# A feature-major SSM and MLP block: the MLP's up-projection in seven products of halves, and gated unit and MLP one half of the tokens after the other

## The chip, the cores and the metric

The kernel runs on one core of a Trainium2 chip. The metric is the device time of one execution in microseconds (us). TensorE (PE, with its weight loads PEld) does the matrix products, VectorE (DVE), ScalarE (ACT) and GpSimd (POOL) the elementwise work, SyncE (SP) issues the transfers between device memory and the core's on-chip memory (SBUF). Products accumulate in PSUM, eight banks of 128 x 512 float32. Each engine executes its own instructions in order and waits for others at semaphores.

## The reference

Two blocks follow each other on a stream x of 2048 tokens by 1024 features in float32. The part that is changed lies in the first block:

```
x = x + a * sigmoid(g)              # a, g = split(y @ w_glu), y: the SSM mixer's gelu output
h = rmsnorm(x, norm_ffn)
a = relu(h @ w1)                    # w1: 1024 x 4096
x = x + (a * a) @ w2                # w2: 4096 x 1024
gate = sigmoid(rmsnorm(x, norm_ple) @ ple_gate_w)
x = x + (p @ ple_w) * gate
return rmsnorm(x, norm_final)       # goes into the second block
```

The second block (band attention, a matrix LSTM, a long convolution, an output projection) and the SSM recurrence itself are not touched.

## The kernel before

The stream lies feature-major: eight tiles x0 to x7 of 128 features by 2048 tokens, worked on in four blocks n of 512 tokens. Every float32 operand of a large product is split into a high and a low float16 part, and each tile of 128 input features takes three matmuls of 128 x 128 by 512 columns: high by high, high weight by low data, low weight by high data (`product`, L252 to L262, matmul on L260). So the third matmul is the first that needs the weight's low part.

A weight tile of 128 x 2048 arrives in two halves `ws` (transfer issued by SP, L1923) and is split by `Weights.prepare` in four quarters: ACT writes a quarter's high part (L1962), then VectorE the low part (`w<-ws,w`, a scalar_tensor_tensor by the helper on L59). That makes five jobs: job q issues the low part of quarter q-1 and the high part of quarter q. When the low part of the second or fourth quarter is issued, that half's buffer goes to the next tile's load. `step(n)` (L245) is called between products and issues up to n jobs of norms that are pending and one job of the weights; `get(i)` issues at once whatever of tile i is left. The order of issue is the order in which each engine works: nothing is scheduled later.

Gated unit (`glu`, L364): a unit (m, n) makes 128 output features for one block, 96 matmuls in two banks; ACT takes the sigmoid (L373), VectorE multiplies (L59) and adds to x (L41), ACT squares for the next norm (L281, L284). For each of the first six tiles m its four blocks n follow one another, and the split of tile m+1 is queued after the first of the four. Two units of tile 0 are begun in the mixer.

MLP (`mlp`, L395): 16 pieces c of 256 hidden features. `up(c, n)` takes 2 x 48 matmuls of two banks; ACT does relu (L414) and the high part of the square (L416), VectorE the square and the low part (L41). `down` of the pair before takes 8 groups of 6 matmuls, each evicted by VectorE into x (L59: `x<-dn,x`). For pieces 2 to 13 all four blocks use a piece's weights in turn.

Per-layer gate (`ple`, L465): 24 matmuls of gate weights (pg) and 6 of the per-layer input (pp) per unit, in two passes over n. Norms of the blocks are jobs: sums of squares through a matmul (nps, L301), rsqrt in small VectorE steps, a matmul that spreads the result over partitions (nsp, L317), and per tile a scalar_tensor_tensor (nt, L59), a cast on ACT (L333) and a subtraction. PSUM is divided among names: four banks "b" (ga, up, pg), three "a" (dn, pp), one "c" (nps, nsp).

## Time and profile before

| what | value |
|---|---|
| median of 3 runs | 3357.24 us (3356.96, 3357.24, 3362.16) |
| span of the profiled execution | 3364.8 us |
| TensorE matmuls busy | 3272.9 us, 97% |
| VectorE busy | 1905.9 us, 57% |
| ScalarE busy | 1059.0 us, 31% |
| moved by DMA | 189.01 MB, mean 56 GB/s |
| gated unit, from its first full unit | 318.9 to 632.8 us |
| MLP | 632.8 to 1971.8 us |

No time of the profiled execution beside its span is given; the span stands for it. Busy times are shares of the whole span, over stages with different limits; the windows by stage below separate them. Matmuls are pipelined, so their recorded durations overlap and the distance from one to the next is what one costs. A number in square brackets on a timeline row is the idle time of that engine before the row, and what ended it.

### The profile page before, as it was taken

The numbers are of one execution on the slowest core, as the hardware profiler recorded it, in microseconds if no ns is written. First come the engines' busy times: TensorE is split into PE (matmuls) and PEld (weight loads), VectorE is DVE, ScalarE is ACT, GpSimd is POOL, SyncE is SP. The second block draws the span as 40 slices with busy tenths as digits, with TensorE's granted clock in tenths as the row PEclk, the third lists the DMA queues.
The fourth block names the chain that finished last, engine by engine and source line by source line (L and its number), as shares of the span: only waits on it lengthen the run. The fifth ranks groups of instructions, "written<-read, shape, count | busy, mean of one in ns | idle before, by whom it ended". The sixth has DMA issues, their size and how long they took to land. (4 is left out here: it accounts for less than half of the span.)

```text
span 3364.8 us, 44052 instructions
## 1 busy us (share of the span) xinstructions
PE 3272.9 (97%) x17524; PEld 1690.9 (50%) x17524; DVE 1905.9 (57%) x4109; ACT 1059.0 (31%) x2293; POOL 165.8 (5%) x162
## 2 busy tenths in 40 slices
PE   7778999999999999999999999999999999999999
PEld 6664444444444444444444444464554445666644
DVE  8995222664444444444444582756657885677742
ACT  8995111321111111111112243331221224555610
POOL 0000111000000000000000223300000000000000
PEclk9888999999999999999999999999999999999999
DMA  4113101100000000000001011032111224322232
GB/s 155 36 49 133 32 26 32 44 1 26 26 26 26 27 30 26 26 26 26 31 26 38 1 51 38 14 129 95 51 66 67 91 88 127 98 80 79 82 141 85
DMA packets 125870, 189.01 MB, mean 56 GB/s; under 512 B 32800, under 2 KB 83936, under 8 KB 121952
## 3 DMA queue, kind: packets, MB, share of 16 engines
q1 hardware_dynamic: 121056, 177.81, 16.3%
q10 hardware_dynamic: 4608, 8.39, 0.6%
q8 instruction: 138, 2.26, 0.3%
q14 instruction: 68, 0.56, 0.1%
HBM read 142.64 MB, written 43.52 MB: 55 GB/s over the span
## 5 line engine op out<-in xcount | busy, mean ns | idle before, releaser
L260 PEld LDWEIGHTS <-w 128*128 128x128 f16 x9792 | 959.0, 98 | 1156.5 <-issue 8.2
L260 PE MATMUL up<-h,w 128*128 128x512 f16 x2880 | 632.1, 379 | 1.7 <-DVE w L59 1.7
L260 PE MATMUL dn<-hid,w 128*128 128x512 f16 x2880 | 632.0, 379 | 1.4 <-DVE x L59 1.4
L59 DVE SCALAR_TENSOR_TENSOR x<-dn,x 128x512 f32<-128x512 f32 x512 | 346.4, 688 | 182.7 <-PE dn L260 180.2
L414 ACT ACTIVATE r<-up 128x512 f32<-128x512 f32 x128 | 76.3, 596 | 975.0 <-PE up L260 974.9
L41 DVE TENSOR_TENSOR q<-r 128x512 f32<-128x512 f32 x128 | 88.5, 692 | 475.3 <-ACT r L414 475.3
L260 PE MATMUL ga<-y,w 128*128 128x512 f16 x1536 | 336.6, 382 | 3.4 <-DVE w L59 2.1
L41 POOL TENSOR_TENSOR ss<-ss,sq 128x512 f32<-128x512 f32 x84 | 113.1, 1347 | 2044.6 <-ACT sq L284 2043.5
L977 PE MATMUL oz<-oz,h 128*128 128x512 f16 x768 | 189.6, 385 | 0.0
L260 PE MATMUL pg<-h,w 128*128 128x512 f16 x768 | 170.8, 379 | 0.0
L59 DVE SCALAR_TENSOR_TENSOR w<-ws,w 128x512 f16<-128x512 f32 x220 | 157.0, 728 | 23.5 <-ACT w L1962 23.5
L1351 PE MATMUL fo<-mx,wo 128*128 128x512 f16 x768 | 167.4, 379 | 0.0
L260 PE MATMUL wide<-w,h 128*128 128x512 f16 x768 | 166.9, 379 | 0.0
L260 PE MATMUL mqk<-h,w 128*128 128x512 f16 x768 | 165.9, 379 | 0.0
L260 PEld LDWEIGHTS <-h 128*128 128x128 f16 x1152 | 112.3, 98 | 99.5 <-DVE gif L59 4.0
L59 DVE SCALAR_TENSOR_TENSOR acc<-u,par,acc 128x512 f32<-128x512 f32 x232 | 159.1, 744 | 0.0
L59 DVE SCALAR_TENSOR_TENSOR sg<-ga,sg 128x512 f32<-128x512 f32 x32 | 22.1, 691 | 214.1 <-ACT sg L373 214.1
L1962 ACT ACTIVATE w<-ws 128x512 f16<-128x512 f32 x220 | 129.2, 616 | 10.3 <-DMA ws<-w 6.2
L1351 PEld LDWEIGHTS <-wo 128*128 128x128 f16 x768 | 75.0, 98 | 88.6
L977 PEld LDWEIGHTS <-h 128*128 128x128 f16 x768 | 71.2, 99 | 68.0 <-issue 3.0
L284 ACT ACTIVATE sq<-x 128x512 f32<-128x512 f32 x84 | 52.7, 630 | 162.7 <-DVE x L41 126.8
L41 DVE TENSOR_TENSOR hid<-q,hid 128x512 f16<-128x512 f32 x128 | 88.6, 692 | 15.4 <-DVE q L41 2.7
(340 smaller groups left out, 3621.5 us busy)
## 6 DMA issues: line engine op xcount, KB each, us to landing
ws<-w SPq DMA_DIRECT2D x64, 512.0 KB
ws<-wd SPq DMA_DIRECT2D x34, 512.0 KB
xu<-xu SPq DMA_DIRECT2D x8, 1024.0 KB
tm<-rz_scr SPq DMA_DIRECT2D x64, 128.0 KB
x<-xT SPq DMA_DIRECT2D x8, 1024.0 KB
ws<-wglu SPq DMA_DIRECT2D x16, 512.0 KB
x_s<-x SPq DMA_DIRECT2D x8, 1024.0 KB
qk_s<-o SPq DMA_DIRECT2D x32, 256.0 KB
```

Of the source, the lines that this page charges most:

```text
L41: f = lambda: (eng or self.nc.vector).tensor_tensor(out=out, in0=in0, in1=in1, op=op)
L59: f = lambda: self.nc.vector.scalar_tensor_tensor(out=out, in0=in0, scalar=s, in1=in1, op0=op0, op1=op1)
L260: self.nc.tensor.matmul(out=ps, lhsT=wk[p], rhs=xk[q], start=(first and i == 0 and j == 0), stop=(last and i == n - 1 and j == 2))
L284: self.nc.scalar.activation(out=sq, in_=x, func=ACT.Square, **kw)
L414: nc.scalar.activation(out=r, in_=ps, func=ACT.Relu, scale=0.5 / WS)
L977: nc.tensor.matmul(out=d["bank", g], lhsT=x[:, k, s], rhs=y[:, c], start=(k == 0 and j == 0), stop=(k == 7 and j == 2))
L1351: self.nc.tensor.matmul(out=self.begun[m, n], lhsT=w[:, x, c], rhs=y[:, k], start=(k == 0 and j == 0), stop=(k == KT - 1 and j == 2))
L1962: nc.scalar.activation(out=hi, in_=src, func=ACT.Copy, scale=scale)
```

## The change

Tokens are worked on in two halves of two blocks. In a half, gated unit, norm and MLP follow each other; wglu, w1 and w2 are loaded and split once for each half. The gated unit's order is half, tile m, block n, and the split of the next tile is queued after the first of the two units of a tile.

The up product of a piece (two blocks of tokens, two halves of 512 input features, two tiles of 128 hidden features) is a product of 2 by 2 blocks, and is made by Strassen's scheme in Winograd's form: seven products of 12 matmuls on sums and differences of operands, in four banks a, c, b, d, with some sums made in the banks and five additions on VectorE. The data's seven combinations are made once for each half by `norm_pair` (`part`, 28 jobs); those of the second half, and one of the first, are parked in device memory and fetched. The weights' seven are made for each piece and half by `combine`: four sums and seven low parts on VectorE, seven high parts on ACT. The square that is subtracted from is made on ACT now. `down` takes both blocks at once: 16 groups of 6 matmuls. The norms ahead of the per-layer gate are made in the middle of the MLP for blocks 0 and 1 (parked and fetched) and in the gate for 2 and 3, and the gate takes blocks 0 and 1 before 2 and 3. Comments are dropped.

The core of the diff; the removed bodies of `glu` and `mlp` stand in the listing above. `fetch` and `fetch_normed` issue transfers from the parking places, `operand` and `combined` name places.

```diff
+        tiles = [(self.a["wglu"][i], WS) for i in range(KT)] * 2
...
-        w = self.weights.get(m)
+        w = self.weights.get(KT * (n // 2) + m)
...
         return ps
     def glu(self, begun):
-        nc = self.nc
+        nc, W = self.nc, self.weights
+        self.places()
         def unit(m, n):
             if m == 0 and n < len(begun):
                 ps = self.gated(n, m, [KT - 1], begun[n])
             else:
-                ps = self.gated(n, m, range(KT), between=lambda: self.step(4))
+                ps = self.gated(n, m, range(KT), between=lambda: self.step(2))
             sg = self.temp(name="sg")
             nc.scalar.activation(out=sg, in_=ps[1], func=ACT.Sigmoid, scale=1 / WS)
             self.stt(sg, ps[0], 1 / WS, sg, ALU.mult, ALU.mult)
             x = self.x[m][:, self.blk(n)]
             self.add(x, x, sg)
             self.squares(m, n, m == 0)
-            self.step(4)
...
+            self.step(2)
+        for half in range(2):
+            for m in range(KT):
+                for n in (2 * half, 2 * half + 1):
+                    unit(m, n)
+                    if n % 2 == 0:
+                        i = KT * half + m + 1
+                        if i < 2 * KT:
+                            W.prepare(i)
+                        else:
+                            self.combined(0)
+            self.norm_pair(half)
...
+    def norm_pair(self, half):
+        nc = self.nc
+        na, nb = 2 * half, 2 * half + 1
...
+        def normed(x, k, n):
+            self.stt(x, self.x[k][:, self.blk(n)], self.gain[:, 0, k:k + 1], self.rb[n % 2], ALU.mult, ALU.mult)
+        def put(x, o, k):
+            away = half or o == 6
+            if away:
+                t = self.parked(at)
+                hi, lo = t[:, 0], t[:, 1]
+            else:
+                hi, lo = (self.operand(o, k, p) for p in range(2))
+            nc.scalar.copy(out=hi, in_=x)
+            def rest():
+                self.sub(lo, x, hi)
+                if away:
+                    dst = self.hop_s[o if half else 7, :, k].rearrange("p (a b) -> p a b", a=2)
+                    nc.sync.dma_start(out=dst, in_=t)
+            low.append(rest)
+        def part(k, q):
+            if low:
+                low.pop()()
+            if q == 0:
+                v["x"] = self.tmp.tile([128, TB], F32, name="nt", tag="n0")
+                v["y"] = self.tmp.tile([128, TB], F32, name="nt", tag="n1")
+            x, y, z = v["x"], v["y"], third
+            if q == 0:
+                normed(x, k, na)
+                put(x, 0, k)
+            elif q == 1:
+                normed(y, k, nb)
+                self.sub(x, y, x)
+                put(x, 1, k)
+            elif q == 2:
+                normed(z, k + 4, nb)
+                put(z, 5, k)
+            elif q == 3:
+                self.sub(y, z, y)
+                put(y, 4, k)
+            elif q == 4:
+                self.sub(x, z, x)
+                put(x, 2, k)
+            elif q == 5:
+                normed(y, k + 4, na)
+                put(y, 3, k)
+            elif q == 6:
+                self.sub(x, y, x)
+                put(x, 6, k)
+        jobs += [lambda k=k, q=q: part(k, q) for k in range(4) for q in range(7)] + [lambda: part(0, 7)]
+        self.pending += [(("pair", half), j) for j in jobs]
...
+        def finish(j, src, r, i, n):
+            t = self.hid[j % 2][i]
+            c = slice(TB * n, TB * n + TB)
+            nc.scalar.activation(out=r, in_=src, func=ACT.Relu, scale=0.5 / WS)
+            nc.scalar.activation(out=t[:, 2, c], in_=r, func=ACT.Square)
+            nc.scalar.activation(out=r, in_=r, func=ACT.Square)
+            later.append(lambda: self.sub(t[:, 3, c], r, t[:, 2, c]))
+        def up(j, steps):
+            ops = W.get(self.at_up[j])
+            u, v = self.rows[2 * (j % 2):2 * (j % 2) + 2]
+            ps = {}
+            for o, name in enumerate("acbadcd"):
+                first = name not in ps
+                if first:
+                    ps[name] = self.bank("b", 4, name="up")
+                for k in range(4):
+                    for p, q in ((0, 0), (0, 1), (1, 0)):
+                        nc.tensor.matmul(out=ps[name], lhsT=ops[o][:, p, 128 * k:128 * k + 128],
+                                         rhs=self.operand(o, k, q), start=(first and k == 0 and p + q == 0),
+                                         stop=(k == 3 and p == 1), skip_group_check=not first)
+                self.step(steps[o])
+                flush()
+                if o == 0:
+                    nc.scalar.copy(out=u, in_=ps["a"])
+                elif o == 2:
+                    self.add(u, ps["b"], u)
+                    self.add(v, ps["c"], u)
+                elif o == 3:
+                    finish(j, ps["a"], self.temp(name="r"), 0, 0)
+                elif o == 4:
+                    self.add(v, ps["d"], v)
+                    finish(j, v, v, 1, 1)
+                elif o == 5:
+                    c = self.temp(name="r")
+                    self.add(c, ps["c"], u)
+                    finish(j, c, c, 0, 1)
+                elif o == 6:
+                    self.add(u, ps["d"], u)
+                    finish(j, u, u, 1, 0)
+        def down(j, between=None):
+            hi, lo = W.get(self.at_dn[j])
+            half, c = j // NPIECE, j % NPIECE
+            for q in range(2):
+                if q and between:
+                    between()
+                for n in range(2):
+                    for m in range(4 * q, 4 * q + 4):
+                        ps = self.bank("a", 3, name="dn")
...
+                        x = self.x[m][:, self.blk(2 * half + n)]
+                        self.stt(x, ps, 4 / WS, x, ALU.mult, ALU.add)
+                        if later:
+                            flush()
+                        if c == NPIECE - 1:
+                            self.squares(m, 2 * half + n, m == 0)
+                        if (m % 2 or j == 2 * NPIECE - 1) and not (q and n and between):
+                            self.step(0 if c < NPIECE - 1 else 1)
...
+        second = lambda j: W.prepare(self.at_dn[j], lambda: w2)
+        self.fetch(6, 7)
+        few, many = (1, 0, 1, 0, 1, 0, 0), (1,) * 7
+        for j in range(2 * NPIECE):
+            c = j % NPIECE
+            if c == 0:
+                self.combined(j + 1)
+            else:
+                second(j - 1)
+            up(j, few if c else many)
+            if c == NPIECE - 1:
+                if j < 2 * NPIECE - 1:
+                    while self.pending:
+                        self.step()
+                    for o in range(7):
+                        self.fetch(o, o)
+                else:
+                    while self.pending:
+                        self.step()
+                    self.fetch_normed()
+            if c:
+                if c < NPIECE - 1:
+                    self.combined(j + 1)
+                down(j - 1, (lambda: second(j)) if c == NPIECE - 1 else None)
+            if c == NPIECE - 1:
+                if j < 2 * NPIECE - 1:
+                    self.combined(j + 1)
+                else:
+                    for i in range(2):
+                        W.prepare(self.at_p + i)
+                    W.prepare(self.at_p + 2, lambda: self.slot(2, [128, 2, 2048], F16, "p0"))
+                down(j)
+                if j < 2 * NPIECE - 1:
+                    self.norm_parked()
+        for n in (2, 3):
+            self.norm(n, 1, late=4)
...
-        order = [(m + e, n) for m in (0, 2) for n in range(NB) for e in range(2)]
+        order = [(m + e, 2 * h + n) for h in range(2) for m in (0, 2) for n in range(2) for e in range(2)]
...
+    def combine(self, i, place):
+        k, nc = self.k, self.k.nc
+        scale = self.tiles[i][1]
+        out = self.ready[i] = []
+        low = []
+        tmp = {}
+        at = lambda r, c: self.loaded[i, c][:, 512 * r:512 * r + 512]
...
+        def source(q):
+            if q in (0, 3, 6):
+                return at(*((0, 0), (0, 1), (1, 1))[q // 3])
+            if q == 1:
+                x = tmp["s"] = new()
+                k.add(x, at(1, 0), at(1, 1))
+            elif q == 2:
+                x = tmp["s"]
+                k.sub(x, x, at(0, 0))
+            elif q == 4:
+                x = new()
+                k.sub(x, at(0, 0), at(1, 0))
+            else:
+                x = tmp["s"]
+                k.sub(x, at(0, 1), x)
+            return x
+        def part(q):
+            if low:
+                low.pop()()
+            if q == 7:
+                return
+            src = source(q)
+            t = place(q)
+            out.append(t)
+            nc.scalar.activation(out=t[:, 0], in_=src, func=ACT.Copy, scale=scale)
+            def rest():
+                k.stt(t[:, 1], src, scale, t[:, 0], ALU.mult, ALU.subtract)
+                j = {4: 0, 6: 1}.get(q)
+                if j is not None:
+                    del self.loaded[i, j]
+                    self.load(i + 1, j)
+            low.append(rest)
+        self.jobs += [(i, lambda q=q: part(q)) for q in range(8)]
```

Three places show how instructions stand. Operands carry buffer numbers; what an instruction waits for stands in brackets.

VectorE at a tile boundary of the gated unit, before: sg and x are a unit's product and sum, w_3638 the low parts of the tile that follows tile 3.

```order
L59 SCALAR_TENSOR_TENSOR sg_3652<-ga0_3600,sg_3652 128x512 [waits Activation_49]
L41 TENSOR_TENSOR x3_2902<-x3_2902,sg_3652 128x512 [waits DVE_49]
L59 SCALAR_TENSOR_TENSOR w_3638<-ws_3459,w_3638 128x512 [waits DMAHW2_49]
L59 SCALAR_TENSOR_TENSOR w_3638<-ws_3459,w_3638 128x512 [waits Activation_49]
L59 SCALAR_TENSOR_TENSOR sg_3715<-ga0_3661,sg_3715 128x512 [waits Activation_49]
L41 TENSOR_TENSOR x3_2902<-x3_2902,sg_3715 128x512 [waits DVE_49]
L59 SCALAR_TENSOR_TENSOR w_3638<-ws_3522,w_3638 128x512 [waits DMAHW3_49]
L59 SCALAR_TENSOR_TENSOR w_3638<-ws_3522,w_3638 128x512 [waits Activation_49]
L59 SCALAR_TENSOR_TENSOR sg_3777<-ga0_3724,sg_3777 128x512 [waits Activation_49]
L41 TENSOR_TENSOR x3_2902<-x3_2902,sg_3777 128x512 [waits DVE_49]
L59 SCALAR_TENSOR_TENSOR sg_3834<-ga0_3784,sg_3834 128x512 [waits Activation_49]
L41 TENSOR_TENSOR x4_2904<-x4_2904,sg_3834 128x512 [waits DVE_49]
```

The last unit of tile 3 is the one of sg_3777, and sg_3834 is the first unit of the next tile. After, at the same boundary; here w_3302 is the tile after tile 3:

```order
L59 SCALAR_TENSOR_TENSOR sg_3257<-ga0_3207,sg_3257 128x512 [waits Activation_49]
L41 TENSOR_TENSOR x3_2902<-x3_2902,sg_3257 128x512 [waits DVE_49]
L59 SCALAR_TENSOR_TENSOR sg_3316<-ga0_3264,sg_3316 128x512 [waits Activation_49]
L41 TENSOR_TENSOR x3_2902<-x3_2902,sg_3316 128x512 [waits DVE_49]
L59 SCALAR_TENSOR_TENSOR w_3302<-ws_3199,w_3302 128x512 [waits DMAHW2_49]
L59 SCALAR_TENSOR_TENSOR w_3302<-ws_3199,w_3302 128x512 [waits Activation_49]
L59 SCALAR_TENSOR_TENSOR w_3302<-ws_3205,w_3302 128x512 [waits DMAHW3_49,Activation_49]
L59 SCALAR_TENSOR_TENSOR w_3302<-ws_3205,w_3302 128x512 [waits Activation_49]
L59 SCALAR_TENSOR_TENSOR sg_3384<-ga0_3334,sg_3384 128x512 [waits Activation_49]
L41 TENSOR_TENSOR x4_2904<-x4_2904,sg_3384 128x512 [waits DVE_49]
```

The four low parts stood behind the second and the third of four units; they stand now behind the second of two, and sg_3384 right after them is the unit that uses the tile.

VectorE where an up product ends and down begins, before (hid and q: squared relu; dn: a bank of down):

```order
L59 SCALAR_TENSOR_TENSOR x7_2910<-dn_9052,x7_2910 128x512 [waits PE_49]
L41 TENSOR_TENSOR q_9088<-r_9086 128x512 [waits Activation_49]
L41 TENSOR_TENSOR hid_9060<-q_9088,hid_9060 128x512 [waits DVE_49,Activation_49]
L41 TENSOR_TENSOR q_9119<-r_9117 128x512 [waits Activation_49]
L41 TENSOR_TENSOR hid_9060<-q_9119,hid_9060 128x512 [waits DVE_49,Activation_49]
L59 SCALAR_TENSOR_TENSOR x0_2328<-dn_9123,x0_2328 128x512 [waits PE_49]
L59 SCALAR_TENSOR_TENSOR x1_2610<-dn_9131,x1_2610 128x512 [waits PE_49]
L59 SCALAR_TENSOR_TENSOR x2_2761<-dn_9139,x2_2761 128x512 [waits PE_49]
```

After, with y2 and y3 the places of the squares, y6 and r those of the sums of banks (up) that enter them:

```order
L41 TENSOR_TENSOR y2_1509<-r_8384,y2_1509 128x512 [waits Activation_49]
L41 TENSOR_TENSOR y6_2656<-up_8388,y6_2656 128x512 [waits DVE_49,PE_49]
L41 TENSOR_TENSOR y3_1803<-y6_2656,y3_1803 128x512 [waits Activation_49]
L41 TENSOR_TENSOR r_8426<-up_8332,y6_2656 128x512 [waits PE_49]
L41 TENSOR_TENSOR y2_1509<-r_8426,y2_1509 128x512 [waits Activation_49]
L41 TENSOR_TENSOR y6_2656<-up_8388,y6_2656 128x512 [waits DVE_49,PE_49]
L59 SCALAR_TENSOR_TENSOR x0_2328<-dn_8448,x0_2328 128x512 [waits PE_49]
L41 TENSOR_TENSOR y3_1803<-y6_2656,y3_1803 128x512 [waits Activation_49]
L59 SCALAR_TENSOR_TENSOR x1_2610<-dn_8457,x1_2610 128x512 [waits PE_49]
L59 SCALAR_TENSOR_TENSOR x2_2761<-dn_8466,x2_2761 128x512 [waits PE_49]
```

Between the last two banks of up and the first evictions of down there were two pairs of square and subtraction; now two sums and three subtractions stand there, and a fourth subtraction between the first two evictions.

TensorE in the per-layer gate, from a spread rstd (nsp) to the next block's sum (nps), both in the bank "c"; before, with 182 rows from the one to the other, of which the first and the last are shown:

```order
L317 MATMUL nsp_13750<-cst_89,r1_92 128x128 [waits PE_49]
...
L260 LDWEIGHTS w_13663
L260 MATMUL pp_13909<-p0_13737,w_13663 128x512
L301 MATMUL nps_13926<-cst_89,ss_2915 128x1 [waits DVE_49,PE_49,Pool_49]
...
L260 LDWEIGHTS w_13515
L260 MATMUL pg_13939<-h1_13364,w_13515 128x512
```

After, 74 rows, of each product the first pair of weight load and matmul:

```order
L333 MATMUL nsp_14393<-cst_89,r1_92 128x128 [waits DVE_49,PE_49]
...
L276 LDWEIGHTS w_14145
L276 MATMUL pp_14413<-p0_14213,w_14145 128x512
...
L276 LDWEIGHTS w_14079
L276 MATMUL pg_14448<-h1_13925,w_14079 128x512
...
L276 LDWEIGHTS w_14145
L276 MATMUL pp_14482<-p0_14213,w_14145 128x512
...
L317 MATMUL nps_14495<-cst_89,ss_2915 128x1 [waits DVE_49,PE_49,Pool_49]
```

The two stand one pg and two pp apart, where several of each stood between them.

## Rows read from the trace of the kernel before

**Rows 1.** The page's first table: busy us, share of the span, count.
```profile
PE 3272.9 (97%) x17524; PEld 1690.9 (50%) x17524; DVE 1905.9 (57%) x4109; ACT 1059.0 (31%) x2293; POOL 165.8 (5%) x162
```
**Rows 2.** The page's groups: busy us, mean ns, then idle us and its releaser.
```profile
L260 PE MATMUL up<-h,w 128*128 128x512 f16 x2880 | 632.1, 379 | 1.7 <-DVE w L59 1.7
...
L59 DVE SCALAR_TENSOR_TENSOR x<-dn,x 128x512 f32<-128x512 f32 x512 | 346.4, 688 | 182.7 <-PE dn L260 180.2
...
L59 DVE SCALAR_TENSOR_TENSOR w<-ws,w 128x512 f16<-128x512 f32 x220 | 157.0, 728 | 23.5 <-ACT w L1962 23.5
...
L1962 ACT ACTIVATE w<-ws 128x512 f16<-128x512 f32 x220 | 129.2, 616 | 10.3 <-DMA ws<-w 6.2
```
**Rows 3.** Windows: length; PE, PEld, DVE, ACT, POOL busy; clock, DMA share, GB/s.
```profile
318.90:632.80 313.90, 313.90 (x1472) 144.41 (x1471) 94.87 (x153) 60.91 (x105) 34.84 (x27) 1.00 0.10 31
632.80:700.00 67.20, 65.19 (x314) 30.82 (x312) 47.70 (x83) 22.95 (x39) 1.27 (x1) 1.00 0.10 32
700.00:1900.00 1200.00, 1200.00 (x5574) 545.63 (x5573) 559.05 (x853) 219.32 (x375) 19.20 (x14) 1.00 0.08 25
1900.00:1971.80 71.80, 70.36 (x343) 34.01 (x342) 51.74 (x95) 25.03 (x44) 16.31 (x11) 1.00 0.07 23
```
**Rows 4.** PE timeline in the MLP: start, us, instructions.
```profile
1001.47 10.52 PE L260 MATMUL up<-h,w 128*128 128x512 f16 x48
1011.83 10.52 PE L260 MATMUL dn<-hid,w 128*128 128x512 f16 x48
```
**Rows 5.** Timeline of all engines in the gated unit.
```profile
401.91 0.60 ACT L373 ACTIVATE sg<-ga 128x512 f32<-128x512 f32 x1 [7.13 <-PE ga L260]
402.54 0.69 DVE L59 SCALAR_TENSOR_TENSOR sg<-ga,sg 128x512 f32<-128x512 f32 x1 [8.94 <-ACT sg L373]
403.26 0.69 DVE L41 TENSOR_TENSOR x<-x,sg 128x512 f32<-128x512 f32 x1
403.87 0.68 DVE L59 SCALAR_TENSOR_TENSOR w<-ws,w 128x512 f16<-128x512 f32 x1
```
**Rows 6.** Timeline of all engines where the gated unit's first tile ends.
```profile
318.77 17.43 PE L260 MATMUL ga<-y,w 128*128 128x512 f16 x80 [0.72 <-ACT sg L373]
...
324.04 0.69 DVE L59 SCALAR_TENSOR_TENSOR w<-ws,w 128x512 f16<-128x512 f32 x1 [1.21 <-ACT w L1962]
```
**Rows 7.** PE timeline, three matmul groups after a wait.
```profile
287.45 10.49 PE L260 MATMUL ga<-y,w 128*128 128x512 f16 x40 [2.10 <-DVE w L59]
...
303.27 1.12 PE L1748 MATMUL yt<-cst,GY 128*128 128x128 f32 x4 [4.01 <-DVE y L41]
...
2206.55 2.87 PE L260 MATMUL av<-wv,h 128*128 128x264 f16 x24 [2.01 <-DVE gif L59]
```
**Rows 8.** Windows of PE: length, busy, granted clock, DMA share, GB/s.
```profile
288.00:290.00 2.00, 2.00 (x6) 0.50 0.53 129
290.00:292.00 2.00, 2.00 (x8) 0.68 0.75 221
...
304.00:306.00 2.00, 2.00 (x7) 0.50 0.23 45
306.00:308.00 2.00, 2.00 (x6) 0.50 0.97 381
...
2206.00:2208.00 2.00, 1.45 (x13) 1.00 0.19 66
```
**Rows 9.** Timelines of PE and DVE in the per-layer gate.
```profile
1998.08 1.13 PE L317 MATMUL nsp<-cst,r 128*128 128x128 f32 x8 [0.84 <-DVE r L59]
1999.04 5.34 PE L260 MATMUL pg<-h,w 128*128 128x512 f16 x24
...
2011.51 0.75 DVE L59 SCALAR_TENSOR_TENSOR nt<-x,gain,nsp 128x512 f32<-128x512 f32 x1
```
**Rows 10.** Timeline of all engines: a low part, then ACT after the load it released.
```profile
1803.22 0.68 DVE L59 SCALAR_TENSOR_TENSOR w<-ws,w 128x512 f16<-128x512 f32 x1
...
1807.45 1.15 ACT L1962 ACTIVATE wp<-ws 128x512 f16<-128x512 f32 x2 [5.25 <-DMA ws<-w]
```

More of the change, by code (lines that the diff above doesn't have):

```diff
@@ L377, in unit @@
             self.squares(m, n, m == 0)
-            self.step(4)
-        for m in range(KT - 2):
-            for n in range(NB):
-                unit(m, n)
-                if n == 0 or (m, n) == (KT - 3, 1):
-                    self.weights.prepare(m + 1 + n)
-        rest = []
-        for n in range(NB):
-            unit(KT - 2, n)
-            unit(KT - 1, n)
-            if n < 2:
-                self.weights.prepare(KT + n)
-            self.norm(n, 0, rest if n else None, late=4)
-        self.pending = [j for j in rest if j[0] == 1] + self.pending + [j for j in rest if j[0] > 1]
@@ new lines, in operand, with parked, spreads, spread @@
+    def operand(self, o, k, p):
+        t, h = self.hop[o][k // 2]
+        return t[:, 2 * h + k % 2, TB * p:TB * p + TB]
+    def parked(self, at):
+        self.npark += 1
+        return at[self.npark % len(at)].bitcast(F16).rearrange("p (a b) -> p a b", a=2)
+    def spreads(self, n, y):
+        r = {}
+        def spread():
+            r["ps"] = self.spread(y)
+        def copy():
+            self.rb[n % 2] = self.tmp.tile([128, TB], F32, name="rb", tag=f"B{6 + n % 2}")
+            self.nc.scalar.copy(out=self.rb[n % 2], in_=r["ps"])
+        return [lambda: None] * 3 + [spread, copy]
@@ new lines, in norm_pair @@
+    def norm_pair(self, half):
+        nc = self.nc
+        na, nb = 2 * half, 2 * half + 1
+        jobs = [lambda: None] * 4
+        self.rb = {}
+        for n in (na, nb):
+            y = self.r1[:, 4 * n:4 * n + 4]
+            jobs += self.rstd_jobs(self.ss[n], self.ones[:, 0:1], D, y) + self.spreads(n, y)
+        at = self.ss[0:1] if half == 0 else self.ss[0:3]
+        third = self.ss[1] if half == 0 else self.ss[3]
+        low, v = [], {}
+        def normed(x, k, n):
[45 more added lines that the diff above has]
+        self.pending += [(("pair", half), j) for j in jobs]
@@ new lines, in fetch, with combined, place @@
+    def fetch(self, o, at):
+        for e, (t, h) in enumerate(self.hop[o]):
+            self.nc.sync.dma_start(out=t[:, 2 * h:2 * h + 2], in_=self.hop_s[at, :, 2 * e:2 * e + 2])
+    def combined(self, j):
+        def place(q):
+            at = (7 * j + q) % 8
+            if at // 4 not in self.ring:
+                self.ring[at // 4] = self.wpool.tile([128, 4, 2, 512], F16, tag=f"w{1 + at // 4}", name="w")
+            return self.ring[at // 4][:, at % 4]
+        self.weights.combine(self.at_up[j], place)
@@ new lines, in norm_parked, with part @@
+    def norm_parked(self):
+        nc = self.nc
+        jobs = [lambda: None] * 4
+        for n in range(2):
+            y = self.r1[:, 4 * n:4 * n + 4]
+            jobs += self.rstd_jobs(self.ss[n], self.ones[:, 0:1], D, y) + self.spreads(n, y)
+        low = []
+        def part(n, k):
+            if low:
+                low.pop()()
+            if n == 2:
+                return
+            x = self.tmp.tile([128, TB], F32, name="nt", tag=f"n{k % 2}")
+            t = self.parked(self.ss[0:2])
+            self.stt(x, self.x[k][:, self.blk(n)], self.gain[:, 1, k:k + 1], self.rb[n], ALU.mult, ALU.mult)
+            nc.scalar.copy(out=t[:, 0], in_=x)
+            def rest():
+                self.sub(t[:, 1], x, t[:, 0])
+                nc.sync.dma_start(out=self.hp_s[n, :, :, k], in_=t)
+            low.append(rest)
+        jobs += [lambda n=n, k=k: part(n, k) for n in range(2) for k in range(KT)] + [lambda: part(2, 0)]
+        self.pending += [(("parked",), j) for j in jobs]
@@ L467, in ple, with fetch_normed @@
+    def fetch_normed(self):
+        for n in range(2):
+            self.h[n] = tuple(self.slot(s, [128, KT, TB], F16, f"h{n}") for s in self.hslots[n])
+            for p in range(2):
+                self.nc.sync.dma_start(out=self.h[n][p], in_=self.hp_s[n, :, p])
     def ple(self):
@@ L472, in gate @@
         def gate(m, n):
-            wg = self.weights.get(base + (3 + m // 2 if m > 1 else 0))
+            wg = self.weights.get(base + (0, 3, 5, 6)[m // 2])
             hi, lo = self.stream(n)
@@ L1889, in ssm @@
             f()
-class Pieces:
-    def __init__(self, part):
-        self.part, self.tiles = part, []
-    def add(self, t):
-        self.tiles.append(t)
-    def __getitem__(self, at):
-        a, b = at[1].start, at[1].stop
-        assert a // 512 == (b - 1) // 512
-        return self.tiles[a // 512][:, self.part, a % 512:a % 512 + b - a]
 class Weights:
@@ L1941, in part @@
             if q == 0:
-                if self.buf(i) is None and not place:
-                    out.extend(Pieces(p) for p in range(2))
-                elif place:
+                if place:
                     t = place()
```

161 lines of the change are left out of this document (72 added, 89 removed).

## The prediction, made before the result

> **What bounds the kernel now.** I read the page's first table, then its groups by line, then the busy times by stage, then the timelines of the places that the change touches. TensorE's matmuls are busy for 97% of the span and no other engine for more than 57% [rows 1]. Within the stage that is rewritten this is sharper: from 700 to 1900 us the row counts 1200.00 us of TensorE in a window of 1200.00, at full clock, and VectorE 559 us, under half [rows 3]. The MLP's groups show no idle time to speak of before 2880 recorded up matmuls, 1.7 us [rows 2]. So in MLP and gated unit a matmul less is time less, and an idle TensorE is time more; whatever else the change does counts only where it makes TensorE wait. One matmul of 512 columns costs its spacing, not its recorded 379 ns: the up group of 48 starts at 1001.47 and the down group behind it at 1011.83, so 10.36/48 = 0.2158 us [rows 4].
>
> **The change, part by part.**
>
> *Matmuls removed.* An up product of a pair of 512-token blocks and 256 hidden columns took 2 x 48 = 96 matmuls; it takes 7 x 12 = 84. There are 32 such pairs: 384 matmuls fewer, 384 x 0.2158 = 82.9 us less. All of it is on the path, as the 1200.00 of 1200.00 shows. The Trainium skill (TensorE: Matmul & The Clock Gate, Back-to-back issue gap) states about 131 ns for each matmul of this size in a sustained stream of weight load and matmul, and about 216 ns for an isolated one. By the first figure the removal would give an estimated 384 x 0.131 = 50.3 us, and the sum below would come out 32.6 higher. This case's trace differs: it has the second figure in a sustained stream [rows 4].
>
> *MLP waits that go.* The two windows at the ends of the MLP show 67.20 - 65.19 and 71.80 - 70.36 us without a matmul [rows 3]: 3.4 us, from norms and weight parts that stood together on VectorE. The norms stand elsewhere now: -3.4.
>
> *The gated unit: weights one unit ahead.* Every tile of wglu is used by two units of 10.36 us in a half instead of four. Its five split jobs are queued after the first of the two, and the second has two places for one job each, the middle of its products and its end. Thus the low part of quarter 0 is issued behind the second unit's sigmoid, its product with the sigmoid and its addition to the stream, and the third matmul of the next unit reads it. The same four instructions stand in the trace in that order today, with three units to spare: sigmoid at 401.91, product 402.54, addition 403.26, low part 403.87 to 404.55 [rows 5]. That is 2.64 us after the sigmoid starts. TensorE needs it two matmuls after it ended, 0.25 us after the sigmoid's start; with some 0.1 to reach it, it waits 2.5. What is queued behind the waiting matmul is the whole next unit. The later quarters are not late: a quarter covers 12 matmuls, 2.59 us, more than one ACT part of 0.62 and one VectorE part of 0.73 [rows 2]. There are 16 such boundaries (15 between tiles, and the last unit to the MLP's first up product, whose operands stand in the same place):
> - ten plain ones: 10 x 2.5 = 25.
> - tile 0 to 1. The two units before it were begun in the mixer and are short. Today TensorE restarts at 318.77 and the low part of tile 1 is ready at 324.04 + 0.69 = 324.73 [rows 6], with nobody waiting. Behind it the first two matmuls of tile 1 would start near 318.7 or soon after, so I take 324.8 - 319.2 = 5.6, net of the 0.72 idle there.
> - five in half 1, where jobs of half 0's norm go ahead of the weight part on VectorE: two with four to six small instructions of the rsqrt, 3.3 and 3.7; three with one or two norm steps, each a VectorE instruction of 0.69 to 0.75 [rows 2, 9] and mostly an ACT cast of about 0.62 between: 5.9, 6.55, 6.55. Sum 26.0.
> Together 56.6. Below: nothing, if the low part gets through earlier than the order says. Above: about 70, if each norm step costs one more VectorE instruction. I take 56.6; the order of instructions leaves little choice.
>
> *Start of the MLP.* The operands of the second w1 tile can be loaded only when the first tile's eight jobs are flushed, about 9.3 us into up(0) by the same 0.62 and 0.73 in turns; release to landing of such a load took 1807.45 - 1803.90 = 3.5 [rows 10]. ACT's copy of the first sum stands behind that tile's first ACT part: 9.3 + 3.5 + 0.62 + 0.6 = 14.0, where the fourth product is due at 10.1 and needs it. That is 4.0, with 1.0 at later products: +5.0 (0 to 8).
>
> *A steady period of the MLP.* 84 matmuls up, 96 down: 38.8 us. VectorE has 40 instructions in it: 16 evictions of down, 4 subtractions and 5 sums of up, 4 low parts of w2, 7 low parts and 4 sums of the combined w1. At 0.69 [rows 2] that is 27.6 us, but 28 of the 40 stand in down, 19.3 of its 20.7: nearly full there, and just ahead of its due times. The tight place is up's end: for each of four quarters relu, square, square on ACT (some 0.62 each, as ACT's weight part [rows 2]) and a subtraction on VectorE, and two of these chains start only with the last two products. In the order now, two subtractions and two sums stand ahead of the first evictions of down, and the last subtraction between them. By these durations the second eviction ends 5.5 us after down's start, and the fifth group of six matmuls, which takes that bank, is due at 4 x 6 x 0.2158 = 5.18. With the 0.1 to reach TensorE: 0.5. In 31 periods 15.5 (0 to 31; the upper end is one more VectorE instruction ahead). The trace of before has such a wait, for an eviction, in the 1.44 us of 1900 to 1971.8 [rows 3].
>
> *Ends of the halves.* The 7 MB fetched in the middle have two downs, 41 us, to land: no wait unless they move slowly, then up to 11. Entry into the per-layer gate: its weights are prepared in the last up, +2.0 with the middle's 0.5.
>
> *Per-layer gate.* The norm of block 2 reads its spread rstd from the only bank "c", whose last reader came 2011.51 + 0.75 - 1998.08 = 14.2 us after the spread's start. The next user of the bank, the sum of block 3, now follows on TensorE after one pp, one pg and one pp: 0.96 + 6 x 0.2158 + 24 x 0.2158 + 6 x 0.2158 = 8.7 us [rows 9]. Wait 5.4, less the 0.84 that is there today: +4.5.
>
> *The clock.* The trace says what a stop costs besides. After the 2.10 wait before 287.45 the granted clock was 0.50 between 288 and 290, which is its lower level, 1.2 of 2.4 GHz: six matmuls in 2 us, where the spacing of [rows 4] gives nine; in the next 2 us it came back. That lost 0.50 x 2 + 0.32 x 2 = 1.64. After 4.01 before 303.27 it was 0.50 to 308, which lost half of 4.7, 2.4. But after 2.01 before 2206.55 it stayed at 1.00 [rows 7, 8]; there matmuls had run closely before, as they do in the gated unit. I take half, 0.82, for each of ten plain waits (0 to 1.64), and 1.9, nearer to the upper end, for each of eight longer ones, the one at up(0) and the one in the per-layer gate among them (0 to 2.4): 8.2 + 15.2 = +23.4 (0 to 35.6).
>
> *Sum.* -82.9 - 3.4 + 56.6 + 5.0 + 15.5 + 2.0 + 4.5 + 23.4 = +20.7. The profiled execution's span is 3364.8, so by it the next one would be 3385.5. That span is 7.6 us above the median of the runs shown, 3357.24; against the median the forecast is 3378.
>
> **Rivals.**
> 1. *The gain arrives whole*: the weight parts get in ahead of the sigmoid's product and the MLP stays gapless: 3357.2 - 82.9 - 3.4 = 3271. For it: VectorE is at 57% and idle for 182.7 us ahead of down's evictions alone [rows 1, 2]. By the Trainium skill (Perfetto Trace Analysis, Identifying the Most-Contended Engine) the engine with the highest occupancy is the one to relieve first; that points here, and the trace agrees for today's kernel. Against: an engine works in order, and [rows 5] is that order. 0.05.
> 2. *Waits in the gated unit only*: no clock loss, no wait in steady MLP: 3378 - 23.4 - 15.5 = 3339. For it: the row at 2206.55; ACT squares could finish earlier. 0.10.
> 3. *A draw*: the waits, and the clock or the MLP's banks but not both in full: 3378 - 23.4 = 3354.6 to 3378 - 15.5 = 3362.5. 0.15.
> 4. *The MLP's VectorE is the bound*: the last subtraction and the sums of weights slip behind evictions, 1.0 wait in each period, each followed by a late bank, and the fetch is late by 11: 3378 + 15.5 + 11 = 3404.5. It decides from about one VectorE instruction (0.69) more per period than fits. For it: the 19.3 of 20.7 above. Against: 27.6 of 38.8 over the whole period, so a delay in down is made good in up. 0.15.
> My forecast, 3378, has 0.55. It is itself on the slower side; the rivals 1 and 2 are on the other.
>
> **Numbers.** A difference under 0.2%, 6.7 us, is no change by what can be measured here: 3350.5 to 3364. Faster: rivals 1 and 2, 0.15. Same: rival 3, 0.15. Slower: 0.70. The range runs from rival 2's 3339 to rival 4's 3404.5, rounded: 3340 to 3405; what is left out is rival 1 and as much at the ends of rivals 2 and 4. The forecast's own range, with clock and MLP each half of the way to a bound (11.7 + 7.8 down, 6.1 + 7.8 up), is 3358 to 3392.
>
> **What would show it.** Right: in the gated unit a TensorE wait of 2 to 3 us for VectorE's weight part at the boundaries of tiles, near 6 at the first and at three of half 1, and stretches with a clock below 1 behind some of them; a wait of half a microsecond for an eviction early in each down; up groups spaced 0.2158. Wrong: a gated unit still near 314 us from the first tile to the last, or a period of the MLP other than 38.8 + 0.5. If the periods measure 40 and more, the bound has moved to VectorE and rival 4 holds; if waits are there and the clock stays at 1.00, rival 3 or 2.

## The result, and the profile after

The changed kernel takes 3381.57 us (median of 4 runs, 3378.7 to 3386.9) against 3357.84 before (4 runs beside it): ratio 1.0069, interval 1.0055 to 1.0084, 23.7 us slower. Predicted were 3378 and a range of 3340 to 3405. One of the seven runs of a later experiment (subtractions behind the evictions) took 5799.25 us at a mean granted clock of 0.68, against 0.97 to 0.98 in the other six; it is left out of that experiment's median, and the one trace kept there, which is of that run, is not used.

One sentence ahead of the prediction is wrong: gated unit, norm and MLP do not follow each other within a half. As the loops in the diff show, the gated unit passes over both halves before the MLP begins. The prediction reckons with that order.

The page's first table and groups, of the kernel after (columns as in [rows 1, 2], which they answer to):

```profile
PE 3217.3 (95%) x17140; PEld 1655.7 (49%) x17140; DVE 2177.2 (64%) x4581; ACT 1326.1 (39%) x2739; POOL 169.6 (5%) x162
...
L276 PE MATMUL dn<-y,w 128*128 128x512 f16 x3072 | 674.5, 379 | 14.3 <-DVE x L59 13.6
L559 PE MATMUL up<-y,w 128*128 128x512 f16 x2688 | 587.0, 379 | 6.6 <-ACT y L565 2.9
...
L276 PE MATMUL ga<-y,w 128*128 128x512 f16 x1536 | 356.0, 395 | 53.8 <-DVE w L59 45.9
```

The same group of ga in the kernel before:

```profile
L260 PE MATMUL ga<-y,w 128*128 128x512 f16 x1536 | 336.6, 382 | 3.4 <-DVE w L59 2.1
```

TensorE is busy for 56 us less and idle for 70 us more. Up has lost its 384 matmuls. Most of the added idle time stands before ga, the gated unit, which the change only reordered: 53.8 us for 3.4. The mean of a ga matmul has risen from 382 to 395 ns: some ran at a lower clock, as the windows below show.

Windows of the kernel after, cut where a stage's first matmul starts (start of the gated unit, first up, first pg, first product of the second block); columns as in [rows 3]:

```profile
284.87:703.13 418.26, 360.35 (x1586) 159.26 (x1585) 145.55 (x217) 99.43 (x161) 36.61 (x27) 0.93 0.17 58
703.13:1981.39 1278.26, 1257.39 (x5826) 570.48 (x5825) 891.12 (x1434) 509.71 (x857) 37.36 (x26) 1.00 0.23 73
1981.39:2149.40 168.01, 162.18 (x763) 76.49 (x762) 77.51 (x154) 58.76 (x103) 53.95 (x40) 0.98 0.10 32
2149.40:3379.00 1229.60, 1210.56 (x7386) 673.53 (x7386) 803.36 (x2088) 409.20 (x1074) 40.27 (x62) 0.99 0.27 88
```

The same cuts in the trace of before, and the experiments that follow:

| stage, us (TensorE busy) | before | after | low part first | split ahead | product made twice | all |
|---|---|---|---|---|---|---|
| gated unit | 348.12 (341.29) | 418.26 (360.35) | 371.60 | 362.99 | 423.20 | 356.16 |
| MLP | 1338.78 (1335.33) | 1278.26 (1257.39) | 1276.71 | 1274.89 | 1358.73 | 1256.07 |
| per-layer gate | 158.84 (157.84) | 168.01 (162.18) | 169.12 | 168.96 | 168.80 | 165.53 |
| second block | 1234.30 (1212.57) | 1229.60 (1210.56) | 1228.70 | 1226.10 | 1225.60 | 1227.60 |

The MLP did become 60.5 us shorter. The gated unit became 70.1 longer: 51.1 of more idle time and 19.1 of busy time for the same matmuls. The gate lost 9.2. The three stages add up to 18.8 us. The second block is the same code, and takes 5 to 9 us more in the trace of before than in the others. The two profiled executions differ by 14.2 us only, and the medians by 23.7: the traced execution of the changed kernel took 3380.83 for a span of 3379.0, so that of before, with its span of 3364.8, took about 3366.6 (an estimate), some 9 more than its median. Differences of a few us between two traces of the same code are thus to be expected: the gated unit, untouched by the third experiment, takes 423.20 there for 418.26.

Waits of TensorE after (us in total, times, longest):

```profile
PE ga L276 <- DVE w L59: 45.9, 15, 6.9
...
PE dn L276 <- DVE x L59: 13.6, 38, 0.7
...
PE ga L276 <- ACT w L2157: 7.9, 4, 6.0
PE nps L317 <- DVE nt L59: 5.7, 1, 5.7
```

All engines at one boundary of two weight tiles, after; it answers to [rows 5] and the order of instructions ahead of the prediction:

```profile
392.59 0.60 ACT L392 ACTIVATE sg<-ga 128x512 f32<-128x512 f32 x1 [7.13 <-PE ga L276]
393.22 0.69 DVE L59 SCALAR_TENSOR_TENSOR sg<-ga,sg 128x512 f32<-128x512 f32 x1 [8.94 <-ACT sg L392]
393.94 0.69 DVE L41 TENSOR_TENSOR x<-x,sg 128x512 f32<-128x512 f32 x1
394.55 0.68 DVE L59 SCALAR_TENSOR_TENSOR w<-ws,w 128x512 f16<-128x512 f32 x1
...
395.30 1.90 PE L276 MATMUL ga<-y,w 128*128 128x512 f16 x8 [2.37 <-DVE w L59]
```

The low part ends at 395.23, 2.64 after the sigmoid's start as in the trace of before; then nobody waited, now the whole unit does. The boundaries of half 0 as TensorE shows them, each group the 96 matmuls of a tile's two units from the third on:

```profile
347.08 20.89 PE L276 MATMUL ga<-y,w 128*128 128x512 f16 x96 [2.31 <-DVE w L59]
370.35 22.58 PE L276 MATMUL ga<-y,w 128*128 128x512 f16 x96 [2.37 <-DVE w L59]
395.30 20.89 PE L276 MATMUL ga<-y,w 128*128 128x512 f16 x96 [2.37 <-DVE w L59]
418.56 20.89 PE L276 MATMUL ga<-y,w 128*128 128x512 f16 x96 [2.37 <-DVE w L59]
441.83 22.58 PE L276 MATMUL ga<-y,w 128*128 128x512 f16 x96 [2.37 <-DVE w L59]
```

The waits are alike, but two groups take 22.58 instead of 20.89. Windows of TensorE's first 4 us behind a wait (length, busy us and count, granted clock, DMA share, GB/s, as in [rows 8]) show why: the mean granted clock was 0.57 in one, so for most of it the clock was at its lower level, 1.2 of 2.4 GHz, and 1.00 in the other.

```profile
370.35:374.35 4.00, 4.00 (x11) 0.57 0.23 46
395.30:399.30 4.00, 4.00 (x19) 1.00 0.21 43
```

One period of the MLP, TensorE, then all engines where up ends in that period:

```profile
1006.94 18.29 PE L559 MATMUL up<-y,w 128*128 128x512 f16 x84
1025.07 5.34 PE L276 MATMUL dn<-y,w 128*128 128x512 f16 x24
1030.77 15.70 PE L276 MATMUL dn<-y,w 128*128 128x512 f16 x72 [0.36 <-DVE x L59]
1046.31 18.29 PE L559 MATMUL up<-y,w 128*128 128x512 f16 x84
```

```profile
1026.11 0.69 DVE L41 TENSOR_TENSOR y<-r,y 128x512 f16<-128x512 f32 x1 [2.02 <-ACT r L546]
1026.72 0.68 DVE L41 TENSOR_TENSOR y<-up,y 128x512 f32<-128x512 f32 x1
1027.32 0.68 DVE L59 SCALAR_TENSOR_TENSOR x<-dn,x 128x512 f32<-128x512 f32 x1
...
1029.42 0.69 DVE L41 TENSOR_TENSOR y<-y,y 128x512 f16<-128x512 f32 x1 [1.42 <-ACT y L546]
1030.03 1.88 DVE L59 SCALAR_TENSOR_TENSOR x<-dn,x 128x512 f32<-128x512 f32 x3
```

Up is 18.13 = 84 x 0.2158. Down stops after 24 matmuls, at its fifth group, until the second eviction ends: this eviction starts at 1030.03 behind the subtraction, which itself waited 1.42 us for ACT's chain, and is done 5.6 us after down's start. Down as a whole takes 21.24 where its matmuls need 20.72: the stop costs 0.52 a period. The row shows 0.36 of it as idle time; the other 0.16 is the end of the last matmul ahead of the stop, whose recorded 0.379 us no next matmul overlaps, less the spacing of 0.2158. The 72 matmuls behind the stop keep their spacing (15.54 us from 1030.77 to 1046.31).

The gate, TensorE; it answers to [rows 9]:

```profile
2006.39 1.46 PE L276 MATMUL pp<-p,w 128*128 128x512 f16 x6
2013.55 1.84 PE L317 MATMUL nps<-cst,ss 128*128 128x1 f32 x8 [5.70 <-DVE nt L59]
2015.25 7.19 PE L276 MATMUL pg<-h,w 128*128 128x512 f16 x24
```

The sum waits for the last nt, as the single bank had it. It takes 1.84 instead of 0.95, and the 24 matmuls behind it 7.19 instead of 5.34: 2.7 us from start to start, the cost of the lower clock.

### The profile page after: what moved, and what is told of

It reads as the page before. It is cut to its first block, busy times and chain, and to the rows that moved or that the text cites. A ratio compares the mean times of both kernels' runs of the same rounds, so it can differ in the third digit from the quotient of the medians.

```text
span 3379.0 us, 44538 instructions
## 1 busy us (share of the span) xinstructions
PE 3217.3 (95%) x17140; PEld 1655.7 (49%) x17140; DVE 2177.2 (64%) x4581; ACT 1326.1 (39%) x2739; POOL 169.6 (5%) x162
## 5 line engine op out<-in xcount | busy, mean ns | idle before, releaser
L276 PE MATMUL dn<-y,w 128*128 128x512 f16 x3072 | 674.5, 379 | 14.3 <-DVE x L59 13.6
L559 PE MATMUL up<-y,w 128*128 128x512 f16 x2688 | 587.0, 379 | 6.6 <-ACT y L565 2.9
L276 PE MATMUL ga<-y,w 128*128 128x512 f16 x1536 | 356.0, 395 | 53.8 <-DVE w L59 45.9
L59 DVE SCALAR_TENSOR_TENSOR w<-ws,w 128x512 f16<-128x512 f32 x356 | 250.3, 719 | 61.7 <-ACT w L2157 60.1
L2208 ACT ACTIVATE w<-sw 128x512 f16<-128x512 f32 x128 | 80.6, 630 | 332.4 <-DVE sw L41 332.4
L2157 ACT ACTIVATE w<-ws 128x512 f16<-128x512 f32 x260 | 153.4, 623 | 55.6 <-PE dn L276 30.0
L276 PEld LDWEIGHTS <-h 128*128 128x128 f16 x1152 | 112.3, 98 | 99.5 <-DVE gif L59 4.0
L41 DVE TENSOR_TENSOR y<-up,y 128x512 f32<-128x512 f32 x128 | 88.2, 689 | 61.2 <-PE up L559 60.1
L41 DVE TENSOR_TENSOR y<-y,y 128x512 f16<-128x512 f32 x64 | 44.3, 693 | 105.4 <-ACT y L546 105.4
```

Of the source, the lines that this page charges most:

```text
L41: f = lambda: (eng or self.nc.vector).tensor_tensor(out=out, in0=in0, in1=in1, op=op)
L59: f = lambda: self.nc.vector.scalar_tensor_tensor(out=out, in0=in0, scalar=s, in1=in1, op0=op0, op1=op1)
L276: self.nc.tensor.matmul(out=ps, lhsT=wk[p], rhs=xk[q], start=(first and i == 0 and j == 0), stop=(last and i == n - 1 and j == 2))
L559: nc.tensor.matmul(out=ps[name], lhsT=ops[o][:, p, 128 * k:128 * k + 128], rhs=self.operand(o, k, q), start=(first and k == 0 and p + q == 0),
L2157: nc.scalar.activation(out=hi, in_=src, func=ACT.Copy, scale=scale)
L2208: nc.scalar.activation(out=t[:, 0], in_=src, func=ACT.Copy, scale=scale)
```

## The experiments

Each is the changed kernel with an edit, the last three with several; times are medians beside runs of the kernel before, whose medians were 3359.16 in the first four, 3357.75 in the next three and 3361.84 in the last.

**The weight's low part first** (is the queue on VectorE the cause?):

```diff
             nc.scalar.activation(out=sg, in_=ps[1], func=ACT.Sigmoid, scale=1 / WS)
+            if n % 2:
+                self.step(2)
             self.stt(sg, ps[0], 1 / WS, sg, ALU.mult, ALU.mult)
...
-            self.step(2)
+            if n % 2 == 0:
+                self.step(2)
```

> Theory (order on VectorE): the gated unit's matmuls wait since the low part of a tile's first quarter stands behind the last unit's product and addition. Issued ahead of them, it is done before it is needed: the ten plain waits of 2.37 us go to under 0.5 (-20 or so), the five of half 1 with norm jobs in front lose some 1.4 each (-7), and about half of the gated unit's 19 us of lost clock comes back: 3381.6 - 20 - 7 - 9 = about 3345. Rival (throughput: VectorE and ScalarE cannot split a tile in two units): the wait stays with another quarter's part, 3370 to 3382.

3333.3 us, ratio to before 0.9927 (0.9913 to 0.994): 48 us less than the changed kernel, where 36 were expected. No work was taken away. The plain waits of half 0 are gone, as TensorE's row shows:

```profile
322.81 163.81 PE L276 MATMUL ga<-y,w 128*128 128x512 f16 x754 [0.50 <-DVE w L59]
```

So the place of the low part in the queue was the cause of these waits, not VectorE's throughput. The gated unit's busy time fell from 360.35 to 348.41: most of these 12 us are lost clock that came back with the waits.

**The split queued ahead of a tile's first unit:**

```diff
-                    unit(m, n)
                     if n % 2 == 0:
                         i = KT * half + m + 1
...
                             self.combined(0)
+                    unit(m, n)
```

> The split of the next tile is queued ahead of the first of a tile's two units instead of behind it, two jobs earlier. Theory (order): no matmul of the gated unit waits for a weight part any more except at the first boundary (6.0 us) and perhaps the first up product; idle time of the stage falls by 45 of its 57.9 and the clock's 19 us come back mostly: 3381.6 - 45 - 17 = about 3320. Rival (throughput): under 20 us won, over 3360.

3321.98 us, 0.9893 (0.9878 to 0.9908). Waits of the gated unit in this kernel:

```profile
PE ga L276 <- DVE w L59: 10.5, 5, 3.3
...
PE ga L276 <- ACT w L2157: 3.4, 1, 3.4
```

Of 53.8 us 13.9 are left: 5.35 at the first boundary, 1.17, 3.28 and 2.65 at three of half 1 behind norm jobs, and one of 1.45 in the mixer's last part. The theory holds in the main; it did not have the three of half 1.

**The third product of each up made twice** (is the saving real?):

```diff
-                for k in range(4):
-                    for p, q in ((0, 0), (0, 1), (1, 0)):
+                for again in range(2 if name == "b" else 1):
+                    for k in range(4):
+                        for p, q in ((0, 0), (0, 1), (1, 0)):
```

> Each up product makes its third product (bank b) twice, the second overwriting the first: 12 matmuls more in each of 32 periods, as many as the change took out. If TensorE bounds the MLP (theory), 384 x 0.2158 = 82.9 us come back: 3381.6 + 82.9 = 3464.5, within 4. If VectorE's 70% had become the bound (rival), the extra 2.6 us a period are slack for it: 40 us or less come back, under 3425.

3461.28 us, 1.0307 (1.0293 to 1.0321): 79.7 us more than the changed kernel. Its MLP, from first up to first pg:

```profile
708.07:2066.80 1358.73, 1340.27 (x6210) 607.97 (x6208) 891.27 (x1434) 509.51 (x857) 37.36 (x26) 1.00 0.21 69
```

TensorE is busy 1340.27 - 1257.39 = 82.88 us longer, and 384 x 0.2158 is 82.87; VectorE's time has not moved (891.27 for 891.12). The saving arrives whole where it was made.

**Subtractions behind the evictions of down:**

```diff
-                flush()
+                if o < 5:
+                    flush()
...
-                        if later:
-                            flush()
+                        if later and (n or m > 1):
+                            later.pop(0)()
```

> The last three subtractions of an up product are issued behind the third, fourth and fifth eviction of the following down instead of ahead of and between the first two. Theory (the chain at up's end makes the eviction of the second bank late): the 38 waits of dn, 13.6 us, go, and the time is 3381.6 - 13 = 3368.5. Rival (VectorE is too full in down): the waits move to later evictions, and the time stays within 4 of 3381.6.

3369.13 us (median of six), 1.0029 (1.0018 to 1.0041): 12.4 us less, for 13 expected. In the run with all edits, below, the waits of dn have gone from 38 in number and 13.6 us to

```profile
PE dn L277 <- DVE x L59: 3.1, 9, 0.7
```

Eight of the nine stand in the very last down and one at the end of the middle's; none is left at a fifth group. The theory holds, and VectorE has room in down.

**Another bank in the gate:**

```diff
-        self.pending += [(n, j) for j in self.rstd_jobs(self.ss[n], self.ones[:, 0:1], D, y)]
+        tag = ("a", 3) if n == 3 else ("c", 1)
+        self.pending += [(n, j) for j in self.rstd_jobs(self.ss[n], self.ones[:, 0:1], D, y, tag=tag)]
```

> The sum of squares of block 3's norm goes into one of the three banks a instead of the single bank c, which block 2's spread rstd holds. Theory (the bank is what it waits for): the wait of 5.7 us before nps goes, and with it the stretch at half clock behind it: 3381.6 - 5.7 - 2 to 3 = about 3373.5. Rival (VectorE is late there anyway, and pp or the spread waits instead): 3379 to 3383.

3378.68 us, 1.0052 (1.0038 to 1.0066): 2.9 less than the changed kernel, where 8 were expected, by medians whose intervals overlap. A miss in the time: 3378.68 lies beside the rival's 3379. TensorE in the gate:

```profile
2009.53 0.95 PE L317 MATMUL nps<-cst,ss 128*128 128x1 f32 x8
2010.34 0.59 PE L276 MATMUL pg<-h,w 128*128 128x512 f16 x2
2014.65 6.40 PE L276 MATMUL pg<-h,w 128*128 128x512 f16 x22 [3.71 <-DVE w L59]
```

The wait before nps is gone, so the bank was what it waited for; but the low part of the gate's second weight tile, behind the same norm jobs on VectorE, was hidden under that wait and is next, as the rival had it for other products. The stage fell by 2.4 us only.

**The split ahead, and three more edits of order:** the split ahead of a tile's first unit as above; weight jobs before norm jobs; tile 1 split in the mixer; up's first copy before its weight job.

```diff
         begun = [self.gated(0)]
+        self.weights.get(1)
...
+        def work(m, n, end=0):
+            for _ in range(2 if m == KT - 1 or (end and n % 2 == 0) else 1):
+                if W.jobs:
+                    W.jobs.pop(0)[1]()
+            for _ in range(min(2, len(self.pending))):
+                self.pending.pop(0)[1]()
...
-                ps = self.gated(n, m, range(KT), between=lambda: self.step(2))
+                ps = self.gated(n, m, range(KT), between=lambda: work(m, n))
...
-            self.step(2)
+            work(m, n, 1)
...
+                if o == 0:
+                    nc.scalar.copy(out=u, in_=ps["a"])
                 self.step(steps[o])
                 flush()
-                if o == 0:
-                    nc.scalar.copy(out=u, in_=ps["a"])
```

> As the run that queued the split ahead of a tile's first unit, and besides: weight jobs go ahead of norm jobs, two at the end of a tile's first unit; tile 1 of wglu is split in the mixer, between the two begun units; in up the copy of the first bank goes ahead of the weight job. Theory (order alone): no wait of the gated unit is left behind its start, nor at up(0): 3322 - 5.4 (first boundary) - 7.1 (three of half 1) - 2.3 (up(0)) - 4 of clock = about 3303. Rival (VectorE cannot hold half 1's norm jobs beside the splits): waits of 2 to 3 us stay there and the time is 3312 to 3322.

3306.61 us, 0.9841 (0.9828 to 0.9855), near the theory's 3303. But not all waits of the gated unit went. The largest that is left stands in half 1, where norm jobs share VectorE with the split:

```profile
603.25 35.10 PE L277 MATMUL ga<-y,w 128*128 128x512 f16 x154 [4.00 <-DVE w L59]
```

Another there is 0.90. So of the rival's picture a part holds.

**All three edits together:**

> All three together: split ahead in the gated unit, subtractions behind the evictions in down, the other bank in the per-layer gate. Theory (three separate waits, each with its own cause): the gains add, 3303 - 11.3 - 8 = about 3284. Rival (what is taken from one wait comes back at the next, VectorE being fuller): 3295 or more.

3291.2 us, 0.9794 (0.9781 to 0.9808): 66.6 us faster than the kernel before. The measured gains add: 3306.61 - 12.4 - 2.9 = 3291.3. The 3284 counted on 8 from the gate's bank, which gave 2.9, and on 3303 from the gated unit.

**The gate's second tile split before the gates, one norm job fewer in each tile's second unit:**

The edit against the run before (the first hunk leaves one norm job fewer between the products of a second unit):

```diff
-            for _ in range(min(2, len(self.pending))):
+            for _ in range(min(2 if end or n % 2 == 0 else 1, len(self.pending))):
...
+        self.weights.get(base + 3)
         order = [(m + e, 2 * h + n) for h in range(2) for m in (0, 2) for n in range(2) for e in range(2)]
```

> As the run with all three changes, and the per-layer gate's second weight tile is split before the gates begin, where VectorE is idle for 7 us; one norm job less in each tile's second unit of the gated unit. Theory (the gate's matmuls wait 3.7 us for that tile's low part once the bank no longer holds them): pg's wait goes, -3.7 and up to -2 of clock, and the 4.9 us of waits in half 1 of the gated unit mostly too: 3291.2 - 3.7 - 4 - 2 = about 3281. Rival (the next thing on VectorE's queue is as late): 3288 to 3292.

3290.14 us, 0.9783 (0.9767 to 0.9799): no difference to the run before. Two of its waits:

```profile
PE up L569 <- ACT sg L401: 4.7, 1, 4.7
...
PE nsp L334 <- DVE r L59: 2.4, 1, 2.4
```

The wait of 3.7 at pg went and the gate is 3.5 us shorter (162.05), but nsp waits 2.4 now. The two waits in half 1, 4.9 us, have become one of 1.0, and the gated unit is 5.1 shorter (351.03); but the first up product now waits 4.7 for a bank, whose reader, the last sigmoid, stands behind norm and weight jobs on ACT, and the MLP is 8.4 longer (1264.45). That the thinned norm jobs pushed that sigmoid back is read from the order on ACT, and no run separates it. What was won in one place was paid in another; the rival's time holds.

## Why the prediction was right

Put to stages, the terms of the prediction's sum are +72.9 for the gated unit, -58.6 for the MLP and +6.4 for the gate; the traces show +70.1, -60.5 and +9.2. So the mechanisms and the size of each stage came out, and not only the total; that 3378 lies within 4 us of 3381.57 is in part luck, since misses of 2 to 3 us cancel and the traces themselves differ by as much.

- **Matmuls removed, -82.9.** Right; the product made twice puts 82.88 of busy time back. The Trainium skill's 131 ns for a matmul in a stream (TensorE: Matmul & The Clock Gate, Back-to-back issue gap) does not hold here: 18.13/84 is 215.8 ns.
- **Gated unit, +56.6 of waits.** Measured 53.8 of idle before ga (1.2 of it in the mixer) and 2.4 at the first up: 55.0. The plain wait is 2.37 for 2.5. The first boundary is 6.0, or 5.3 without the 0.72 that stood there before, for 5.6. The three with norm steps are 6.2, 6.95 and 7.7 (a first stop of 0.6 to 0.8 with each) for 5.9, 6.55 and 6.55; the two with rsqrt steps 3.37 and 2.05 for 3.3 and 3.7, and one reckoned as plain is 1.48. The misses cancel.
- **Clock.** I took half a fall for each plain wait, and in the gated unit 18.8 of the 23.4. Nine stretches behind waits there took longer than their matmuls at 0.2158, by 18.5 in all (an estimate from the timeline). Of the eight plain waits of the stage four were followed by a fall, at a cost of 1.5 to 1.7 us each (22.58 - 20.89 = 1.69 for two). The half was a guess between rows with a fall and a row without one, so that it fits is luck. At up(0), where 1.9 were reckoned, no fall followed.
- **MLP.** Start: 4.2 (2.88 + 0.99 + 0.33) for 5.0. Period: 0.52 for 0.5, at the fifth group of down and behind the chain that was named; but the prediction's own figures, 5.5 + 0.1 - 5.18, make 0.42, which was written as 0.5, so a part of this fit is luck. It came in 28 downs (14.6 us), where 31 were counted (15.5). End: the waits in the last down of each half beside that stop are 1.4 in the middle and 2.7 at the end, for 2.0 together, and come from evictions and weight parts on VectorE, not from a transfer. Together the stage fell by 60.5, where the terms give some 59.
- **Gate.** The wait is 5.7 for 5.4. The clock behind it cost 2.7 for 1.9. TensorE is busy 4.3 us longer in the stage, and the other 1.7 of that is no loss: of the sums of squares and the spreads (nps and nsp, 0.81 and 0.89 from start to start) one pair more stands in the gate, and fewer in the stages ahead. So the stage lost 9.2 for 6.4.
- **Rivals.** That VectorE becomes the MLP's bound (rival 4) is excluded by the product made twice and by the late subtractions. Rivals 2 and 3 left out the clock, the MLP's stops or both, and both are there. The whole gain (rival 1), 3271, was hidden by the gated unit's order alone for the most part: with that order mended it is 3306.61, with all edits 3291.2.

## What to carry to other kernels

A change that saves work in one stage is priced at every stage whose loop order it alters. Halving the uses of a weight tile halves the time in which the next one can be made ready, and what decided here was not the share of busy time but where the preparing instruction stood in its engine's queue: ahead of or behind work that waits for the very engine it is to feed. When a wait is taken away, look in the same place for the next one, which the first has hidden.

## What the runs showed of the hardware that was not expected

Eight waits of 2.3 to 2.4 us between stretches of some 96 matmuls are alike in length, with matmuls in close order ahead of and behind each, and four of them were followed by a stretch at 1.2 GHz and four were not. In the two further runs that leave the gated unit as it is (product made twice, other bank) it was four of eight as well, in one of them at another tile: falls behind the waits that end at 370, 442, 490 and 681 us in the changed kernel, at 375, 423, 495 and 686 with the product made twice, where everything stands 4.9 us later. So in these three traces it was not the same waits that cost the clock, but as many of them; why one does and another does not stays open. The stops of 0.36 us in the MLP cost none: the granted clock of that window is 1.00.

A stop delays the work by more than the idle time that the timeline shows, also at full clock: the 0.36 us before down's fifth group lengthened down by 0.52, since the idle time is counted from the recorded end of a matmul, 0.379 us behind its start, and the matmuls follow one another every 0.2158.
